# Latent attention scores as three float32r products with operands split one head ahead, and the first norm's steps moved behind the last scale and shift piece

## The chip, the cores and the metric

The kernel runs on one core of one Trainium2 chip. The metric is device microseconds of one execution, as a median over runs. In the rows PE is the matrix engine (TensorE), DVE is VectorE, ACT is ScalarE, POOL is GpSimd, and SP issues most transfers. Matrix products accumulate in eight PSUM banks of 512 float32 columns.

## What is computed

One inference step of a two-layer backbone. 128 context tokens and 256 latent tokens go through the same layers, together 384 columns. A modulation (shift, scale and gate per layer, three times each) is computed from a conditioning vector. Cut to what matters:

```
x += 0.5 * gate1 * SwiGLU1(mod(RMSNorm(x)))
h  = mod(RMSNorm(x));  u = h @ W_in
z  = sig(g_conv)*P_conv(conv) + sig(g_na)*P_na(NA) + sig(g_mla)*P_mla(MLA)
x += gate2 * (z @ W_o)
x += 0.5 * gate3 * SwiGLU2(mod(RMSNorm(x)))
...
prob = softmax(scale * q k^T (+ bias)); o = prob v
```

MLA is attention with 8 heads whose keys are 64 expanded plus 32 rotated dimensions; NA is neighbourhood attention with 8 heads of 64 dimensions and a bias table. Latent queries see 256 latent and 128 cached keys; context queries see the 128 context keys. Everything is float32 in and out.

## The kernel before

The tokens lie in the free dimension (384 columns), features in the partitions. A **dense product** is made of float32r matmuls: the weight is split into a high part (cast on ACT, L320) and a low part (subtraction on DVE, L321), the activation likewise (`split`: cast on ACT L367, subtraction on DVE L368), and three products are added, high·high (L362), low·high activation (L363), high·low weight (L364). Weights come in chunks of 512 KB with 8 blocks of 128x128; `Weights.split` splits a chunk `ahead` chunks (3 as a rule) before PE uses it, and it is called where PE begins a new chunk. `pair` holds the same three products for the FFN's gate and up tiles (L661).

The program is scheduled by hand: on each engine the instructions stand in the order in which the code issues them, and an engine waits at the first whose operands are missing. So the place of a step in the code is its place in each engine's queue.

`first_group` (from L535) computes the first six output tiles of a sublayer with k, the block of 128 features, as the outer loop. It works on features that are not normalised yet, and meanwhile the eight `norm_tile`s of the normalised activation are made in steps: multiply by the inverse RMS (DVE L524), scale and shift (ACT L527, two instructions), then `split` into `hh` and `hl` (ACT L367, DVE L368). `STEPS` says behind which k which tile's next step is issued. In the first sublayer of all, `START_STEPS` says it, and there `start(c)` (c = 0 to 3) also finishes a quarter of the scale and shift vectors: DVE copies it out of PSUM (L402), PE transposes it (L407), DVE reduces it (L408), and ACT and DVE scale two tiles of x by it (L516, L518). `start(3)` stands inside k = 5.

In `attention`, `mla_query(h)` makes a head's query (DVE L957 multiplies it by the rotation) and, for even heads, two heads' keys (ACT copies L962, L963). `scores(heads)` multiplies queries and keys (PE L874 for 2x128 latent queries by 384 keys, L876 for the context), takes the maxima (DVE L889, for NA L885 with the bias), their negative (L890), the exponentials (ACT L895), the reciprocals of the sums (DVE L897) and the probabilities (DVE L902). `transposed` turns them (PE L911, ACT L912), `values` multiplies by v (PE L927, L930; DVE L931). The loop issues, for head i of MLA: scores(i), the query of head i+2, a piece of the convolution (dense tiles on PE, DVE L834 to L850), values of an earlier pair, and transposed(i-1). The NA heads follow in pairs, a pair's two heads side by side in 64-row tiles of PE; `na_values` (L818 to L820) stands behind the first pair. In this kernel the scores are float32 matmuls of q and k as they are; one such matmul leaves two records in the trace.

Of the kernel before, what the change touches and what calls it, by code (L numbers as in the profile page):

```python
# [18 lines left out]
P = 128  # L19
# [27 lines left out]


STEPS = {2: (0, 1, 0, 2, 1, 0), 3: (3, 2, 1, 4, 3, 2), 4: (5, 4, 3, 6, 5, 4), 5: (7, 6, 5, 7), 6: (6,), 7: (7,)}
START_STEPS = {4: (0, 1, 0, 2, 1, 0), 5: (3, 2, 1, 4, 3, 2), 6: (5, 4, 3, 6, 5, 4), 7: (7, 6, 5, 7, 6, 7)}  # L50


START = {0: 0, 1: 1, 3: 2, 5: 3}
# [222 lines left out]
class Weights:  # L276
# [53 lines left out]
    def next(self, n=1):  # L330
        u, b = divmod(self.n, BPC)
        if b == 0:
            self.split(u + self.ahead)
            self.parts.pop(u - 1, None)
        assert b + n <= BPC
        self.n += n
        return tuple(x[:, b * P:(b + n) * P] for x in self.parts[u])
# [7 lines left out]
def step_kernel(ctx, tc, xT, cc, wst, cst_d, vec_d, rpb, ck_na, cv_na, ck_kv, ck_r, yd, o_k, o_v, o_ckv, o_kr):  # L345
# [8 lines left out]
    def wt(n=TOK):  # L354
        return base.tile([P, TOK], F32, tag="w", bufs=8, name="w")[:, :n]

    def small(n, dtype=F32):
        return base.tile([P, 16], dtype, tag="small", bufs=16, name="small")[:, :n]
# [122 lines left out]
    nc.scalar.copy(ones_r, ones)  # L481

    def split_squares():
        sums[:] = [base.tile([P, TOK], F32R, tag=x, name=x) for x in ("sqh", "sql")]
        split(sums[0], sums[1], sumsq[0])

    def add_square(t, last=False):
# [45 lines left out]
    def first_group(l, idx, pool=None):  # L533

        steps = START_STEPS if pool else STEPS
        at_rms = 3 if pool else 1
        if pool:  # L540
            cz = pool.tile([P, KD, 32], F32, name="cz")
            nc.vector.memset(cz, 0.0)
            nc.scalar.activation(cz[:, :, 0:2], vec[:, V_C:V_BADA].rearrange("p (k v) -> p k v", v=2), AF.Silu)
        rest = {}

        def start(c):
            for finish in rest.pop(c):
                finish()
            scales(0, 0, slice(2 * c, 2 * c + 2))
            if c == 0:  # L550
                W.split(0)
            for t in (2 * c, 2 * c + 1):
                scaled(t)
            if c < 2:
                add_square(2 * c)
                add_square(2 * c + 1)

        out = [ps() for _ in range(GROUP)]
        for k in range(KD):
            if pool and k in START:  # L560
                rest[START[k]] = [start_quarter(m, START[k], cz) for m in (1, 0)]
                if k == 0:
                    start(0)
            for j, o in enumerate(out):
                if pool and k % 2 and k < KD - 1 and j == 2:
                    W.prepare()
                    start(k // 2 + 1)
                mm3(o[:, :TOK + 2], W.next(), (hh[:, k, :], hl[:, k, :]), k == 0, k == KD - 1)
            if pool and k == 2:
                for t in range(4, KD):  # L570
                    add_square(t)
                split_squares()
            if k == at_rms:
                rb = inverse_rms()
                tiles = [norm_tile(l, idx, t, rb) for t in range(KD)]
            for t in steps.get(k, ()):
                next(tiles[t])
        b = small(2 * GROUP)
        for j, o in enumerate(out):
            nc.vector.tensor_copy(b[:, 2 * j:2 * j + 2], o[:, TOK:TOK + 2])  # L580
        return out, rb, b
# [145 lines left out]
    def attention(l, h, pool, o_conv, o_na, o_mla):  # L727
# [126 lines left out]

        probs, probsT, queries, mla, na = {}, {}, {}, {}, {}

        def scores(heads):


            near = heads[0] >= 8  # L860
            scale = 1.0 if near else MLA_SCALE
            operands, tiles = [], []
            for i in heads:
                if near:
                    r, j = slice(64 * (i % 2), 64 * (i % 2) + 64), i % 8 // 2
                    operands.append((qna[r, j, :], kna[r, j, :]))
                else:
                    operands.append((queries.pop(i), mla["k"][:, i % 4, :]))
                s = ps(), ps()
                tiles.append((s[0][:, :TOK], s[1][:, :TOK], s[0][:, TOK:]))  # L870
            for j in range(3):
                for (q, k), s in zip(operands, tiles):
                    if j < 2:
                        nc.tensor.matmul(s[j], q[:, NCTX + j * P:NCTX + (j + 1) * P], k[:, NCTX:], start=True, stop=True)  # L874
                    else:
                        nc.tensor.matmul(s[2], q[:, :NCTX], k[:, :NCTX], start=True, stop=True)  # L876
            cols = [slice(0, TOK), slice(TOK, 2 * TOK), slice(2 * TOK, 2 * TOK + NCTX)]
            n = 3 * len(heads)
            mx, nm, sm, rs = small(n), small(n), small(n), small(n)
            for a, (i, s) in enumerate(zip(heads, tiles)):  # L880
                probs[i] = pool.tile([P, 2 * TOK + NCTX], F32, tag="prob", bufs=2, name="prob")
                for j in range(3):
                    m = mx[:, 3 * a + j:3 * a + j + 1]
                    if near and j < 2:
                        nc.vector.tensor_tensor_reduce(  # L885
                            out=probs[i][:, cols[j]], in0=s[j], in1=biases[i % 8][:, j, :], scale=1.0, scalar=-3.0e38,
                            op0=ALU.add, op1=ALU.max, accum_out=m)
                    else:
                        nc.vector.tensor_reduce(m, s[j], axis=AX.X, op=ALU.max)  # L889
            nc.vector.tensor_scalar(nm, mx, -scale, None, op0=ALU.mult)  # L890
            for a, (i, s) in enumerate(zip(heads, tiles)):
                for j in range(3):
                    c = 3 * a + j
                    src = probs[i][:, cols[j]] if near and j < 2 else s[j]
                    nc.scalar.activation(probs[i][:, cols[j]], src, AF.Exp, bias=nm[:, c:c + 1], scale=scale,  # L895
                                         accum_out=sm[:, c:c + 1])
            nc.vector.reciprocal(rs, sm)  # L897
            for a, i in enumerate(heads):
                for j in range(3):
                    c = 3 * a + j  # L900
                    p = probs[i][:, cols[j]]
                    nc.vector.tensor_scalar(p, p, rs[:, c:c + 1], None, op0=ALU.mult)  # L902
                biases.pop(i - 8, None)
# [40 lines left out]
        def mla_query(hd):  # L944


            if hd == 0:
                k = mla["k"] = pool.tile([P, 4, ALLK], F32, tag="A8", bufs=3, name="kmla")

                kr = ps()  # L950
                nc.tensor.matmul(kr, cst[0:64, C_PM:C_MASK], R, start=True, stop=True)
                nc.scalar.copy(k[0:64, 0::2, :], kr[0:64, :].unsqueeze(1).to_broadcast([64, 2, ALLK]))
                nc.scalar.copy(k[64:128, 1::2, :], kr[64:128, :].unsqueeze(1).to_broadcast([64, 2, ALLK]))
            o = dense_tile((cqh, cql), 2)
            q = pool.tile([P, TOK], F32, tag="qmla", bufs=3, name="qmla")
            cs = cst[:, C_CSO:C_CSK] if hd % 2 else cst[:, C_CSE:C_CSO]
            nc.vector.tensor_tensor(q, o[:, :TOK], cs, op=ALU.mult)  # L957
            queries[hd] = q
            if hd % 2 == 0:
                o = ps()  # L960
                mm3(o, W.next(), (ckh, ckl), True, True)
                nc.scalar.copy(mla["k"][64:128, hd % 4, :], o[64:128, :])  # L962
                nc.scalar.copy(mla["k"][0:64, hd % 4 + 1, :], o[0:64, :])  # L963

        mla_values()
        mla_query(0)
        mla_query(1)
        for i in range(8):
            scores([i])
            if i + 2 < 8:  # L970
                mla_query(i + 2)
            if i == 6:
                bias([0, 1])
            for _ in range(FILL[i]):
                next(conv)
            if i >= 3 and i % 2:
                values(i - 3)
            if i >= 1:
                transposed(i - 1)
        for i in range(8, 18, 2):  # L980
            if i > 8:
                transposed(i - 2)
                transposed(i - 1)
            if i < 16:
                scores([i, i + 1])
                if i < 14:
                    bias([i - 6, i - 5])
            if i == 8:
                transposed(7)
                na_values()  # L990
            for _ in range(FILL[i]):
                next(conv)
            values(i - 2)
# [64 lines left out]
```

## Time and profile before

| | us |
|---|---|
| median of 3 runs | 1905.04 (1904.65 to 1905.15) |
| the profiled execution | 1904.49 |
| its span | 1902.7 |
| PE busy | 1875.3 (99%) |
| DVE busy | 1312.3 (69%) |
| ACT busy | 813.2 (43%) |

The mean granted clock of PE was 0.996. A timeline row gives start, duration (of the group, if it counts several), engine, line, operation, output and inputs, count, and in brackets the idle time before it with what ended that. A group of instructions that run one behind the other is one row. Rows overlap: the next PE row begins before the last has drained, so the price of a matmul is the distance between starts, not its duration.

### The profile page before, as it was taken

What the parts mean: (1) busy time and instruction counts of PE and PEld (TensorE: products, weight loads), DVE (VectorE), ACT (ScalarE), POOL (GpSimd) and SP (SyncE); (2) the same over time, 40 slices, a digit from 0 to 9 for tenths busy, and PEclk for the clock granted to TensorE, in tenths of its full rate; (3) what the DMA queues carried; (4) which work ended last, traced back from release to release, by engine and by line L of the source; (5) the groups of instructions that cost most, each with busy time, mean ns of one, the idle gap of its engine ahead of it and who ended that gap; (6) DMA issues with size and microseconds to landing.
All of it is one profiled execution on the core that took longest, in us unless ns stands there. A gap on an engine that the chain in (4) does not pass through costs nothing.

```text
span 1902.7 us, 27717 instructions
## 1 busy us (share of the span) xinstructions
PE 1875.3 (99%) x10804; PEld 1824.2 (96%) x10804; DVE 1312.3 (69%) x2235; ACT 813.2 (43%) x1358; POOL 45.1 (2%) x79
## 2 busy tenths in 40 slices
PE   6999999999999999999999999999999999999998
PEld 5999999988999999999999999998789999999997
DVE  6788767665877778776778776666578766744433
ACT  4633334655533354333354333356554334633332
POOL 0000000013000000000000000000220000000000
PEclk9999999999999999999999999999999999999999
DMA  7567554423455535655535664533335643343331
GB/s 304 190 230 227 198 178 151 130 79 111 144 191 174 196 106 181 219 198 188 178 122 195 206 207 169 186 108 118 101 100 175 205 163 122 112 140 122 127 125 63
DMA packets 85523, 306.12 MB, mean 161 GB/s; under 512 B 9616, under 2 KB 11248, under 8 KB 85264
## 3 DMA queue, kind: packets, MB, share of 16 engines
q1 hardware_dynamic: 83376, 297.21, 46.8%
q0 software_dynamic: 1728, 5.41, 1.0%
q8 instruction: 84, 1.38, 0.3%
q10 hardware_dynamic: 288, 1.74, 0.3%
q14 instruction: 47, 0.39, 0.1%
HBM read 301.53 MB, written 2.79 MB: 160 GB/s over the span
## 4 chain that ended last, share of the span: by engine, by line
PE 93%; DVE 3%; ACT 2%; issue 1%; DMA 0%; SPq 0%; DVEq 0%; ACTq 0%
PE ps L661 34%; PE ps L363 18%; PE ps L362 18%; PE ps L364 18%; PE ps L874 1%; PE ps L911 1%; PE ps L927 1%; PE ps L820 1%; PE ps L818 1%; PE ps L819 1%; ACT w L527 1%; ACT prob L895 0%; DVE lo L321 0%; DVE small L889 0%; ACT hi L320 0%
## 5 line engine op out<-in xcount | busy, mean ns | idle before, releaser
L321 DVE TENSOR_TENSOR lo<-raw,hi 128x1024 fp32r<-128x1024 f32 x414 | 504.8, 1223 | 245.6 <-ACT hi L320 243.9
L320 ACT CAST hi<-raw 128x1024 fp32r<-128x1024 f32 x414 | 429.7, 1046 | 361.6 <-PE ps L363 230.8
L362 PE MATMUL ps<-hh,hi 128*128 128x384 f32 (+1 forms) x960 | 327.4, 341 | 1.9 <-ACT hh L516 1.4
L363 PE MATMUL ps<-hl,hi 128*128 128x384 f32 (+1 forms) x960 | 326.5, 340 | 2.4 <-DVE hl L368 1.8
L364 PE MATMUL ps<-hh,lo 128*128 128x384 f32 (+1 forms) x960 | 325.9, 339 | 0.0
L424 DVE SCALAR_TENSOR_TENSOR junk<-rawa,cb 128x1024 bf16<-128x1024 f32 x256 | 312.9, 1222 | 4.4
L661 PE MATMUL ps<-hl,hi 128*128 128x384 f32 x1216 | 312.6, 338 | 0.0
L661 PE MATMUL ps<-hh,lo 128*128 128x384 f32 x1216 | 312.1, 338 | 0.0
L661 PE MATMUL ps<-hh,hi 128*128 128x384 f32 x1216 | 310.3, 336 | 0.0
L364 PE MATMUL ps<-ah,lo 128*128 128x384 f32 x704 | 237.8, 338 | 0.0
L362 PE MATMUL ps<-ah,hi 128*128 128x384 f32 x704 | 237.8, 338 | 0.0
L363 PE MATMUL ps<-al,hi 128*128 128x384 f32 x704 | 237.8, 338 | 0.0
L661 PEld LDWEIGHTS ps<-hh,lo 128*128 128x128 f32 x1216 | 221.7, 188 | 0.0
L661 PEld LDWEIGHTS ps<-hh,hi 128*128 128x128 f32 x1216 | 221.3, 188 | 0.0
L661 PEld LDWEIGHTS ps<-hl,hi 128*128 128x128 f32 x1216 | 220.1, 188 | 0.0
L362 PEld LDWEIGHTS ps<-hh,hi 128*128 128x128 f32 x960 | 182.2, 190 | 5.5 <-ACT hh L516 1.8
L363 PEld LDWEIGHTS ps<-hl,hi 128*128 128x128 f32 x960 | 181.7, 189 | 3.6 <-DVE hl L368 2.3
L364 PEld LDWEIGHTS ps<-hh,lo 128*128 128x128 f32 x960 | 182.1, 190 | 0.0
L362 PEld LDWEIGHTS ps<-ah,hi 128*128 128x128 f32 x704 | 132.2, 188 | 0.0
L364 PEld LDWEIGHTS ps<-ah,lo 128*128 128x128 f32 x704 | 132.2, 188 | 0.0
L363 PEld LDWEIGHTS ps<-al,hi 128*128 128x128 f32 x704 | 132.2, 188 | 0.0
L638 ACT ACTIVATE w<-ps 128x384 f32<-128x384 f32 x76 | 37.2, 490 | 165.4 <-PE ps L661 165.4
(193 smaller groups left out, 1909.1 us busy)
## 6 DMA issues: line engine op xcount, KB each, us to landing
raw<-wst SPq DMA_DIRECT2D x414, 512.0 KB, 3.4
rawa<-wst SPq DMA_DIRECT2D x128, 512.0 KB, 3.4
s<-wst SPq DMA_DIRECT2D x16, 512.0 KB, 10.0
bias<-rpb POOLq DMA_DIRECT2D x16, 256.0 KB, 3.3
X<-xT SPq DMA_DIRECT2D x4, 384.0 KB, 9.5
y<-X SPq DMA_DIRECT2D x3, 512.0 KB, 3.9
cb<-cc ACTq DMA_DIRECT2D x1, 1024.0 KB, 6.8
cst<-cst ACTq DMA_DIRECT2D x1, 672.0 KB, 4.8
```

Source lines behind the costliest of these rows:

```text
L320: nc.scalar.copy(hi, raw)
L321: nc.vector.tensor_tensor(lo, raw, hi.bitcast(F32), op=ALU.subtract)
L362: nc.tensor.matmul(out, w[0], x[0], start=start, stop=False)
L363: nc.tensor.matmul(out, w[0], x[1], start=False, stop=False)
L364: nc.tensor.matmul(out, w[1], x[0], start=False, stop=stop)
L424: nc.vector.scalar_tensor_tensor(junk, w, 1.0, cb[:, v], op0=ALU.mult, op1=ALU.mult, accum_out=mods[l][:, m, t, v:v + 1])
L527: nc.scalar.activation(h[:, sl], h[:, sl], AF.Identity, bias=mods[l][:, 3 * idx, t, s:s + 1], scale=A[0][:, t, s:s + 1])
L638: nc.scalar.activation(s, g[:, :TOK], AF.Silu)
L661: nc.tensor.matmul(o[:, :TOK], w[part], y, start=k == 0 and i == 0, stop=k == KD - 1 and i == 2)
L818: nc.tensor.matmul(o, xh, wh, start=k == 0, stop=False)
L819: nc.tensor.matmul(o, xl, wh, start=False, stop=False)
L820: nc.tensor.matmul(o, xh, wl, start=False, stop=k == KD - 1)
```

## The change

Four edits. The norm steps of the very first group (`START_STEPS`) begin after k = 5 instead of after k = 4. In the other first groups the chunk split that stood between the last norm steps is put behind the loop (`W.ahead`). The sums of squares use the ring of work tiles (`wt`). The latent scores are made of three float32r products each; a new `prepare(heads)` casts and subtracts query (256 columns) and key (384 columns) one head, or one pair, ahead of its scores. The context scores stay as they are.

```diff
-START_STEPS = {4: (0, 1, 0, 2, 1, 0), 5: (3, 2, 1, 4, 3, 2), 6: (5, 4, 3, 6, 5, 4), 7: (7, 6, 5, 7, 6, 7)}
+START_STEPS = {5: (0, 1, 0, 2, 1, 0, 3), 6: (2, 1, 4, 3, 2, 5, 4, 3, 6), 7: (5, 4, 7, 6, 5, 7, 6, 7)}
...
-        sums[:] = [base.tile([P, TOK], F32R, tag=x, name=x) for x in ("sqh", "sql")]
+        sums[:] = [wt().bitcast(F32R) for _ in range(2)]
...
+            if not pool and k == KD - 2:
+                W.ahead = AHEAD - 1
...
+        if not pool:
+            W.ahead = AHEAD
...
+        def prepare(heads):
+            i = heads[0]
+            if i >= 8:
+                q, k = qna[:, i % 8 // 2, :], kna[:, i % 8 // 2, :]
+                rows = [slice(64 * e, 64 * e + 64) for e in range(2)]
+            else:
+                q, k = queries.pop(i), mla["k"][:, i % 4, :]
+                rows = [slice(0, P)]
+            qs = [pool.tile([P, NLAT], F32R, tag="sq", bufs=4, name="sq") for _ in range(2)]
+            ks = [wt().bitcast(F32R) for _ in range(2)]
+            split(*qs, q[:, NCTX:])
+            split(*ks, k[:, NCTX:])
+            ready[i] = [(q[r], k[r], [x[r] for x in qs], [x[r] for x in ks]) for r in rows]
...
-            for j in range(3):
-                for (q, k), s in zip(operands, tiles):
-                    if j < 2:
-                        nc.tensor.matmul(s[j], q[:, NCTX + j * P:NCTX + (j + 1) * P], k[:, NCTX:], start=True, stop=True)
-                    else:
-                        nc.tensor.matmul(s[2], q[:, :NCTX], k[:, :NCTX], start=True, stop=True)
+            for j in range(2):
+                for n, (a, b) in enumerate(((0, 0), (1, 0), (0, 1))):
+                    for (_, _, q, k), s in zip(operands, tiles):
+                        nc.tensor.matmul(s[j], q[a][:, j * P:(j + 1) * P], k[b], start=n == 0, stop=n == 2)
+            for (q, k, _, _), s in zip(operands, tiles):
+                nc.tensor.matmul(s[2], q[:, :NCTX], k[:, :NCTX], start=True, stop=True)
...
         mla_query(0)
+        prepare([0])
         mla_query(1)
         for i in range(8):
+            prepare([i + 1] if i < 7 else [8, 9])
             scores([i])
...
+            if i < 14:
+                prepare([i + 2, i + 3])
             if i < 16:
                 scores([i, i + 1])
```

How this moves instructions, at three places. On DVE in the very first group, around k = 5 (L524 is a norm step, the two L402 the copies out of PSUM that `start(3)` begins with); before:

```order
L321 TENSOR_TENSOR lo_403<-raw_186,hi_402 128x1024
L524 TENSOR_TENSOR w_426<-X_64,rb_389 128x384
L524 TENSOR_TENSOR w_428<-X_64,rb_389 128x384
L524 TENSOR_TENSOR w_432<-X_64,rb_389 128x384
L368 TENSOR_TENSOR hl_74<-w_426,hh_73 128x384
L402 COPY w_447<-ps_438 128x256
L402 COPY w_458<-ps_449 128x256
L321 TENSOR_TENSOR lo_467<-raw_242,hi_466 128x1024
```

and of the change:

```order
L321 TENSOR_TENSOR lo_403<-raw_186,hi_402 128x1024
L402 COPY w_435<-ps_426 128x256
L402 COPY w_446<-ps_437 128x256
L321 TENSOR_TENSOR lo_455<-raw_242,hi_454 128x1024
L408 TENSOR_REDUCE mod0_71<-ps_460 128x4
L389 TENSOR_TENSOR mod0_71<-mod0_71,vec_65 128x4
```

Three multiplications and one subtraction that stood ahead of the copies now stand behind the whole of `start(3)`.

On ACT at the end of the mixers' first group (L527 and L367 belong to the last two norm tiles, L320 is a chunk's cast); before:

```order
L527 ACTIVATE w_3104<-w_3104,mod0_71,A_2086 128x128
L527 ACTIVATE w_3104<-w_3104,mod0_71,A_2086 128x256
L320 CAST hi_3124<-raw_2994 128x1024
L367 CAST hh_73<-w_3074 128x384
L367 CAST hh_73<-w_3104 128x384
L320 CAST hi_3173<-raw_3048 128x1024
```

and of the change:

```order
L527 ACTIVATE w_3104<-w_3104,mod0_71,A_2086 128x128
L527 ACTIVATE w_3104<-w_3104,mod0_71,A_2086 128x256
L367 CAST hh_73<-w_3074 128x384
L367 CAST hh_73<-w_3104 128x384
L320 CAST hi_3167<-raw_2994 128x1024
L320 CAST hi_3173<-raw_3048 128x1024
```

The chunk's cast changed places with the last two casts of the norm; the subtractions on DVE follow the same order.

On DVE in attention, from the first query to the first probabilities' sum (`sq` and `w` are the low parts of query and key; lines of the change are 17 higher from `scores` on); before:

```order
L957 TENSOR_TENSOR qmla_3477<-ps_3470,cst_66 128x384
L321 TENSOR_TENSOR lo_3490<-raw_3353,hi_3489 128x1024
L957 TENSOR_TENSOR qmla_3498<-ps_3485,cst_66 128x384
L889 TENSOR_REDUCE small_3505<-ps_3500 128x1
L889 TENSOR_REDUCE small_3505<-ps_3501 128x1
L889 TENSOR_REDUCE small_3505<-ps_3500 128x1
L890 TENSOR_SCALAR small_3506<-small_3505 128x3
```

and of the change:

```order
L974 TENSOR_TENSOR qmla_3477<-ps_3470,cst_66 128x384
L368 TENSOR_TENSOR sq_3486<-qmla_3477,sq_3485 128x256
L368 TENSOR_TENSOR w_3488<-kmla_3465,w_3487 128x384
L321 TENSOR_TENSOR lo_3498<-raw_3353,hi_3497 128x1024
L974 TENSOR_TENSOR qmla_3506<-ps_3493,cst_66 128x384
L368 TENSOR_TENSOR sq_3509<-qmla_3506,sq_3508 128x256
L368 TENSOR_TENSOR w_3511<-kmla_3465,w_3510 128x384
L906 TENSOR_REDUCE small_3525<-ps_3516 128x1
L906 TENSOR_REDUCE small_3525<-ps_3517 128x1
L906 TENSOR_REDUCE small_3525<-ps_3516 128x1
L907 TENSOR_SCALAR small_3526<-small_3525 128x3
```

Two subtractions per head stand ahead of the maxima of the head before; on ACT two casts stand likewise ahead of its exponentials.

## Rows read from the trace of the kernel before

**Rows 1.** The page: busy time of each engine.
```profile
PE 1875.3 (99%) x10804; PEld 1824.2 (96%) x10804; DVE 1312.3 (69%) x2235; ACT 813.2 (43%) x1358; POOL 45.1 (2%) x79
```

**Rows 2.** Timeline of PE in the first group.
```profile
47.29 1.12 PE L407 MATMUL ps<-cst,w 128*128 128x128 f32 x4 [5.36 <-DVE w L402]
```

**Rows 3.** Timeline of DVE in the same stretch.
```profile
43.40 1.49 DVE L524 TENSOR_TENSOR w<-X,rb 128x384 f32<-128x384 f32 x3
...
46.82 0.75 DVE L402 COPY w<-ps 128x256 f32<-128x256 f32 x2
...
61.52 1.23 DVE L321 TENSOR_TENSOR lo<-raw,hi 128x1024 fp32r<-128x1024 f32 x1
```

**Rows 4.** Timeline of ACT in the same stretch.
```profile
44.05 1.86 ACT L527 ACTIVATE w<-w,mod,A 128x128 f32<-128x128 f32 x4 [7.94 <-DVE w L524]
...
60.44 2.94 ACT L320 CAST hi<-raw 128x1024 fp32r<-128x1024 f32 x3
```

**Rows 5.** Windows: length, busy and count of PE, PEld, DVE, ACT, POOL; PEclk, DMA.
```profile
46.00:52.00 6.00, 4.71 (x16) 4.68 (x17) 5.22 (x16) 3.88 (x9) 0.00 (x0) 0.50 0.28 96
...
373.00:430.00 57.00, 56.30 (x332) 47.60 (x332) 38.57 (x98) 32.13 (x80) 4.83 (x8) 1.00 0.23 76
430.00:500.00 70.00, 70.00 (x431) 60.12 (x430) 45.18 (x113) 38.58 (x93) 15.25 (x25) 1.00 0.35 113
```

**Rows 6.** The chain of waits: its longest piece (start, us).
```profile
58.81 159.85 PE ps L661 x912
```

**Rows 7.** Timeline of all engines at the end of the mixers' first group.
```profile
339.16 1.03 ACT L320 CAST hi<-raw 128x1024 fp32r<-128x1024 f32 x1
...
340.08 0.33 PE L364 MATMUL ps<-hh,lo 128*128 128x384 f32 x1
340.10 0.92 ACT L367 CAST hh<-w 128x384 fp32r<-128x384 f32 x2
...
340.66 0.44 PE L362 MATMUL ps<-hh,hi 128*128 128x384 f32 x1 [0.24 <-ACT hh L367]
...
341.37 1.02 DVE L368 TENSOR_TENSOR hl<-w,hh 128x384 fp32r<-128x384 f32 x2
...
341.97 0.44 PE L363 MATMUL ps<-hl,hi 128*128 128x384 f32 x1 [0.87 <-DVE hl L368]
```

**Rows 8.** Timeline of PE: scores of an MLA head, then of an NA pair.
```profile
410.19 1.46 PE L874 MATMUL ps<-kmla,qmla 128*128 128x384 f32 x4
411.48 0.38 PE L876 MATMUL ps<-kmla,qmla 128*128 128x128 f32 x2
...
450.29 1.56 PE L874 MATMUL ps<-kna,qna 64*128 64x384 f32 x8
```

**Rows 9.** Waits of DVE from 373 to 430 us: in total, times, longest.
```profile
DVE small L897 <- ACT prob L895: 13.2, 8, 1.7
DVE lo L321 <- ACT hi L320: 3.7, 4, 2.3
DVE small L889 <- PE ps L876: 1.2, 1, 1.2
```

**Rows 10.** Timeline of DVE: subtractions of 128 and of 384 columns.
```profile
363.04 0.28 DVE L368 TENSOR_TENSOR ckl<-ckc,ckh 128x128 fp32r<-128x128 f32 x1
...
365.29 1.02 DVE L368 TENSOR_TENSOR cql<-w,cqh 128x384 fp32r<-128x384 f32 x2
```

**Rows 11.** Timeline of ACT: the second key copy of the first two heads.
```profile
373.26 0.58 ACT L963 COPY kmla<-ps 64x512 f32<-64x512 f32 x1
```

**Rows 12.** Timeline of DVE: maxima of the first and of the last MLA head.
```profile
376.43 1.21 DVE L889 TENSOR_REDUCE small<-ps 128x1 f32<-128x384 f32 x3
...
425.52 1.21 DVE L889 TENSOR_REDUCE small<-ps 128x1 f32<-128x384 f32 x3
```

**Rows 13.** Timeline of PE: the first NA pair's scores, and the last MLA head's transposes.
```profile
428.26 0.59 PE L874 MATMUL ps<-kna,qna 64*128 64x384 f32 x1 [0.69 <-ACT prob L895]
...
429.37 0.96 PE L911 MATMUL ps<-cst,prob 128*128 128x128 f32 x7
```

More of the change, by code (lines that the diff above doesn't have):

```diff
@@ L855, in attention @@
         probs, probsT, queries, mla, na = {}, {}, {}, {}, {}
+        ready = {}
+        def prepare(heads):
[11 more added lines that the diff above has]
+            ready[i] = [(q[r], k[r], [x[r] for x in qs], [x[r] for x in ks]) for r in rows]
         def scores(heads):
@@ L861, in scores @@
             scale = 1.0 if near else MLA_SCALE
-            operands, tiles = [], []
+            operands, tiles = ready.pop(heads[0]), []
             for i in heads:
-                if near:
-                    r, j = slice(64 * (i % 2), 64 * (i % 2) + 64), i % 8 // 2
-                    operands.append((qna[r, j, :], kna[r, j, :]))
-                else:
-                    operands.append((queries.pop(i), mla["k"][:, i % 4, :]))
                 s = ps(), ps()
                 tiles.append((s[0][:, :TOK], s[1][:, :TOK], s[0][:, TOK:]))
-            for j in range(3):
-                for (q, k), s in zip(operands, tiles):
-                    if j < 2:
-                        nc.tensor.matmul(s[j], q[:, NCTX + j * P:NCTX + (j + 1) * P], k[:, NCTX:], start=True, stop=True)
-                    else:
-                        nc.tensor.matmul(s[2], q[:, :NCTX], k[:, :NCTX], start=True, stop=True)
+            for j in range(2):
[4 more added lines that the diff above has]
+                nc.tensor.matmul(s[2], q[:, :NCTX], k[:, :NCTX], start=True, stop=True)
             cols = [slice(0, TOK), slice(TOK, 2 * TOK), slice(2 * TOK, 2 * TOK + NCTX)]
```

## Prediction

> **What bounds the kernel now.** I read the page first: PE is busy for 1875.3 us, 99% of the span [rows 1]. So there is little idle time to win, and a change gains only where it closes one of PE's gaps or takes time out of PE's own work. I then looked along PE's timeline for gaps, and at what ended each. The longest of the first group is at 47.29 us: PE stands 5.36 us until DVE has copied a quarter of the modulation out of PSUM [rows 2]. Two short ones stand at the end of the mixers' first group, at 340.66 and 341.97, and both recur in the second layer [rows 7]. The third place is attention, 373 to 430 us. There PE is busy 56.30 of 57 us and DVE only 38.57 [rows 5], which looks as if PE alone counted. The waits of DVE say otherwise: of its 18 us idle, 13.2 are eight waits for the exponentials, and only one wait of 1.2 us is for scores from PE [rows 9]. So seven of the eight heads' maxima begin when DVE's own queue lets them, with the scores already there. DVE with ACT's exponentials is a second loop as long as PE's, in the order of a hand schedule; PE runs ahead of it by small margins. What is put into that loop moves every later head.
>
> **The very first group.** Before, the copies L402 begin at 46.82, behind three L524 that begin at 43.40 and a subtraction that waits for ACT [rows 3]. Now they take the place of the first L524: 46.82 - 43.40 = 3.42 us earlier, and with them L407, so PE's idle time falls from 5.36 to 1.94. Before, the granted clock was 0.50, the lower level, from 46 to 52 us, behind the idle stretch [rows 5]; I take it that after 1.94 us it does not fall. The gain does not last to the end of the norm, however. While PE stood, ACT did scale and shift of two tiles, 1.86 us [rows 4], and a cast, .41 (what the second of two adds [rows 7]), together some 2.2; this work now comes behind `start(3)`, on an engine with the other norm tiles queued, and the chunk cast that PE needs next stands behind all of them (the x3 group at 60.44 [rows 4]). Of the 3.4 - 2.2 = 1.2 the new pipe's first multiplication takes .65 before ACT can begin (43.40 to 44.05 [rows 3, 4]). That cast and the subtraction at 61.52 [rows 3] so come about .6 earlier. PE needs them for the fifth k of its next pair of tiles. Before, the group ended at 58.81 [rows 6] and four k took 4 x 6 x .175 = 4.2 us (.175 = 159.85/912 [rows 6]): 63.0, later than the subtraction's end, 61.52 + 1.23 = 62.75, so there was no wait, and the fifth k ended at 63.0 + 1.05 = 64.05. Now PE would be at the fifth k some 5 us earlier and waits about 3.3 for the cast and again for the low part, at 62.75 - .6 = 62.15; two more passes, .35, and the fifth k ends at 62.5. Net: **-1.5 us**. Bounds: -5 (the chunk is no obstacle) and +1.5 (the clock falls in the new idle time: six us at half speed lose 3.0 [rows 5]).
>
> **The other first groups.** In the mixers a chunk's cast begins at 339.16 and the last two norm casts only at 340.10; behind them DVE does the chunk's low part first, and the last L368 only from 341.37 [rows 7]. Start to start PE loses (340.66 - 340.08 - .17) + (341.97 - 340.66 - .17) = .41 + 1.14 = 1.55, and .1 in the slower first passes behind each gap. With the casts at 339.16, both high parts are there by 340.1 and the low ones by 340.8, when PE wants them at 340.2 and 340.4 for one k after the other; I count the gaps as gone. The split that is put behind has three chunks of lead. In the FFN's first groups PE has no such gap, so nothing is won there. **-1.65 per layer, -3.3.** Bounds -3.5 and -1.5.
>
> **PE's saving in the scores.** Four records of an MLA head take 411.48 - 410.19 = 1.29 us start to start, .3225 each [rows 8]; six float32r passes of 384 columns take 6 x .175 = 1.05. So a head saves .24. An NA pair's eight records last 1.56 where an MLA head's four last 1.46 [rows 8]: the two 64-row tiles run side by side. If the float32r ones do too, a pair saves .24. Over 16 heads and 8 pairs that is 5.8 us at most. A float32 matmul is two records, .645, which is 3.7 float32r passes. The Trainium skill, "FP8 and Floating Point Precision", section TensorE Precision Notes, says that float32 takes four passes (high and low parts, all four products); by it the saving would be .70 - .525 = .175 instead of .12 a matmul, 48 x .055 = 2.7 us more, and the sum 1910.7; the row decides, and it says .645.
>
> **The price of the preparation.** Two subtractions of 384 take 1.02, the second adding .47 to the first's .55; one of 128 takes .28, .20 without its drain [rows 10]. So 256 columns cost .34 and a head's two subtractions **.81 us** on DVE. On ACT two casts of 384 take .92 [rows 7], so a head's two about .8, in the time in which it waits for the maxima anyway; that I cost at nothing, except at head 0. There query and keys exist only from 373.26 + .58 on [rows 11], so the first casts end about 374.6 and the key's low part about 375.2, where PE began the scores about 373.6: +1.1 for PE with its saving counted. On DVE two preparations, 1.62, and this delay stand ahead of head 0's maxima: about +2.1 on 376.43 [rows 12]. Each of the next seven heads finds one more preparation ahead of it: 7 x .81 = 5.7. The only idle time in front of maxima, 1.2 us [rows 9], takes up about .9. So head 7's maxima move from 425.52 [rows 12] by 2.1 + 5.7 - .9 = 6.9 us, and its exponentials and probabilities with them. PE already waited .69 for those exponentials at 428.26 (a PSUM bank), and its transposes of head 7 come right behind at 429.37 [rows 13]: they have no margin and move by 6.9. One output tile of `na_values` takes a bank that the first pair's maxima free, .45 more. PE: **+7.35 per layer, +14.7**; its own saving in the eight heads disappears in these waits. The bounds: nothing but the saving less head 0's wait, 8 x .24 - 1.1 = -.8 per layer, and 8 x .81 + 2.1 = +8.6. I take the upper part because DVE shows no other idle time that a preparation could fall into: those 13.2 us stand inside each head's softmax, behind the place of the preparation. Where it goes ahead of the maxima, it cannot use them. Among the NA pairs DVE and ACT are less loaded against PE's dense work (45.18 and 38.58 of 70 us, PE 70.00 [rows 5]), so there only PE's saving shows: three pairs, -.7 per layer, **-1.5**.
>
> **The sum.** 1904.49 - 1.5 - 3.3 + 14.7 - 1.5 = 1912.9 for the profiled execution; the median of the runs stands .55 above it, so **1913.4**.
>
> **The rivals.** *PE alone counts* (faster, .15): the subtractions fall into DVE's 18 idle us and delay nobody. For it: PE is busy 98.8% of that stretch [rows 5]. Against it: the waits [rows 9]. It decides at the point where DVE idles ahead of the maxima, waiting for PE: if the scores come last there, a preparation is free. Then -1.5 - 3.3 - 5.8 + 2 x 1.1 = -8.4: 1896.6. *The 64-row float32r tiles don't run side by side* (.10): a pair then needs 12 x .175 = 2.10 against 1.05, +1.05 for six pairs beyond the waits, +6.3: 1919.7. No row shows such a pair; the float32 ones speak against it [rows 8]. *The clock falls again* in the first group or in an attention wait of 2 us or more (.08): +3.0, 1916.4. *Half the delay* is taken up by L321's waits for ACT, 3.7 us in that stretch [rows 9] (.07): 1913.4 - 7.35 = 1906.
>
> **How the numbers follow.** The forecast has .60, with 1909 to 1917 as its own range (the bounds of the first two edits, and one us per layer in the loop). The range 1904 to 1921 takes in all but the rival in which PE alone counts. A measurement of this kernel can tell .2%, 3.8 us, from no change: faster is below 1901.2, slower above 1908.8. Faster has .15; the half delay and the forecast's low end make .10 for the same; slower has .75.
>
> **What would show it.** In the profile of the changed kernel L407 should begin near 43.9 with about 1.9 us idle, and PE should wait some 3 us for `lo` of L321 in the first pair behind the group; the two gaps of the mixers' group should be gone. In attention, DVE should wait for PE's scores in none or one head, PE should wait several times for ACT's exponentials or copies and for DVE's probabilities, together about 8 us per layer, and a head's maxima should begin behind its successor's subtractions. If DVE waits for PE in most heads, the loop theory is wrong. If NA scores of a pair take 2.1 us, the second rival is right.

## The result, and the profile after

The changed kernel takes **1919.38 us** (median, 1918.76 to 1920.08) against 1904.85 us of the kernel before beside it: a ratio of 1.0077, with an interval of 1.006 to 1.0095. It is slower, by 14.5 us where the forecast was 8.5; the time lies within the range of 1904 to 1921, near its upper end, and above the forecast's own 1909 to 1917. (Of the kernel with float32 scores below one execution is left out: it took 2293 us at a granted clock of .75 from end to end.)

The page of the changed kernel: PE's work hardly grew, its share of the span fell. The last line is the chain of work that ended last; below it stands that of the kernel before, in which DVE and ACT had less.

```profile
span 1918.0 us, 27947 instructions
...
PE 1879.9 (98%) x10868; PEld 1836.0 (96%) x10868; DVE 1334.7 (70%) x2283; ACT 830.5 (43%) x1406; POOL 45.4 (2%) x79
...
PE 89%; DVE 5%; ACT 3%; DMA 1%; issue 1%; SPq 0%; DVEq 0%; ACTq 0%
```
```profile
PE 93%; DVE 3%; ACT 2%; issue 1%; DMA 0%; SPq 0%; DVEq 0%; ACTq 0%
```

To see where the 15.3 us of span went, I took five stretches between the same instructions of PE in each trace. The marks are the first product with the sums of squares (L448), the FFN's first down product, the two small products at the head of attention (`R`, L951, now L968), the start of the last `values` of layer 0, and the same two places of layer 1.

| stretch, us | before | changed | difference | forecast |
|---|---|---|---|---|
| first group and FFN | 183.37 | 183.45 | +.1 | -1.5 |
| down products and mixers' first group | 151.07 | 149.40 | -1.67 | -1.65 |
| attention, layer 0 | 125.94 | 135.99 | +10.05 | +6.6 |
| between the two layers' attention | 802.29 | 800.65 | -1.64 | -1.65 |
| attention, layer 1 | 125.83 | 134.91 | +9.08 | +6.6 |

(The forecast's 6.6 is 7.35 for the loop less .72 for three pairs.) The five differences add up to 15.9; the other -.6 lies ahead of the first mark (-.4) and behind the last (-.2). So the split's edit gave what it was to give, the start gave nothing, and attention cost half as much again as forecast.

**The very first group.** PE's and ACT's timelines of the changed kernel:

```profile
43.45 0.77 PE L407 MATMUL ps<-cst,w 128*128 128x128 f32 x4 [1.94 <-DVE w L402]
...
60.52 0.62 PE L665 MATMUL ps<-hh,hi 128*128 128x384 f32 x2 [2.05 <-ACT hi L320]
...
61.78 0.69 PE L665 MATMUL ps<-hh,lo 128*128 128x384 f32 x1 [0.26 <-DVE lo L321]
```
```profile
59.43 2.93 ACT L320 CAST hi<-raw 128x1024 fp32r<-128x1024 f32 x3
```

The idle time in front of L407 is 1.94 us, as worked out, where it was 5.36 [rows 2]; the wait for the chunk has come in its place, as the prediction had it (2.05 and .26 us, where it said 3.3), and the chunk's cast begins 1.0 us earlier than before [rows 4]: the .6 of the forecast, and .4 by which this execution was ahead already at the products with the sums of squares (34.71 against 35.12 us). What the sum had put at nothing is the clock. The windows over the two waits:

```profile
43.50:48.00 4.50, 4.50 (x18) 4.38 (x19) 4.21 (x15) 1.49 (x4) 0.00 (x0) 0.62 0.73 228
60.00:66.00 6.00, 5.23 (x20) 4.88 (x21) 5.71 (x14) 3.31 (x6) 0.00 (x0) 0.72 0.84 304
```

Mean granted clocks of .62 and .72 mean that a part of each window, behind its wait of 2 us, ran at the lower of the two levels.

**The mixers' first group.** ACT's timeline: the last two norm casts now stand ahead of the chunks', and PE waits for nothing from 330 to 366 us.

```profile
338.85 0.91 ACT L367 CAST hh<-w 128x384 fp32r<-128x384 f32 x2
339.66 2.00 ACT L320 CAST hi<-raw 128x1024 fp32r<-128x1024 f32 x2
```

**Attention.** DVE's waits from 371 to 439 us, then PE's:

```profile
DVE small L914 <- ACT prob L912: 13.2, 8, 1.7
DVE sq L368 <- ACT sq L367: 2.4, 3, 1.7
DVE lo L321 <- ACT hi L320: 1.8, 4, 0.5
```
```profile
PE ps L944 <- ACT probT L929: 4.1, 2, 2.5
PE ps L891 <- ACT prob L912: 2.0, 1, 2.0
PE ps L891 <- ACT w L367: 0.9, 1, 0.9
PE ps L891 <- DVE sq L368: 0.8, 1, 0.8
PE ps L362 <- ACT prob L912: 0.3, 1, 0.3
```

DVE still waits eight times for the exponentials, 13.2 us, to the tenth what it was [rows 9]: the preparation used none of that time. The one wait for PE's scores is gone. PE in turn waits 8.1 us, where it waited .7. The maxima of the first and the last head on DVE's timeline, with the last head's preparation:

```profile
376.60 1.21 DVE L906 TENSOR_REDUCE small<-ps 128x1 f32<-128x384 f32 x3
...
431.14 0.42 DVE L368 TENSOR_TENSOR sq<-qna,sq 128x256 fp32r<-128x256 f32 x1
431.47 0.55 DVE L368 TENSOR_TENSOR w<-kna,w 128x384 fp32r<-128x384 f32 x1
431.94 1.21 DVE L906 TENSOR_REDUCE small<-ps 128x1 f32<-128x384 f32 x3
```

Attention begins 2.0 us earlier (367.56 against 369.56), so head 0 is late by 376.60 - 376.43 + 2.0 = 2.2 us and head 7 by 431.94 - 425.52 + 2.0 = 8.4 [rows 12]. Forecast were 2.1 and 6.9.

### The profile page after: what moved, and what is told of

Read it like the earlier page. It is cut to its first block, busy times and chain, and to the rows that moved or that the text cites. A ratio compares the mean times of both kernels' runs of the same rounds, so it can differ in the third digit from the quotient of the medians.

```text
span 1918.0 us, 27947 instructions
## 1 busy us (share of the span) xinstructions
PE 1879.9 (98%) x10868; PEld 1836.0 (96%) x10868; DVE 1334.7 (70%) x2283; ACT 830.5 (43%) x1406; POOL 45.4 (2%) x79
## 3 DMA queue, kind: packets, MB, share of 16 engines
q8 instruction: 85, 1.39, 0.3%
## 4 chain that ended last, share of the span: by engine, by line
PE 89%; DVE 5%; ACT 3%; DMA 1%; issue 1%; SPq 0%; DVEq 0%; ACTq 0%
PE ps L665 33%; PE ps L362 17%; PE ps L363 17%; PE ps L364 17%; ACT prob L912 1%; DVE small L906 1%; DMA s<-wst 1%; PE ps L928 1%; DVE lo L321 1%; PE ps L944 1%; PE ps L822 1%; PE ps L823 1%; PE ps L824 1%; ACT hi L320 1%; DMA X<-xT 1%
## 5 line engine op out<-in xcount | busy, mean ns | idle before, releaser
L320 ACT CAST hi<-raw 128x1024 fp32r<-128x1024 f32 x414 | 429.9, 1046 | 368.5 <-PE ps L363 229.6
## 6 DMA issues: line engine op xcount, KB each, us to landing
s<-wst SPq DMA_DIRECT2D x16, 512.0 KB, 10.1
```

The source lines that it names most:

```text
L320: nc.scalar.copy(hi, raw)
```

## The experiments

Two theories. **The loop:** what costs the time is the place of the subtractions on DVE, ahead of the maxima, in a loop that is as long as PE's. **The rival:** the new products, ACT's casts or the clock cost it, wherever the subtractions stand. Eight kernels tell them and the parts apart; three more try what follows. "Attention" below is the stretch of the table, layer 0 and layer 1.

**The start's order alone** (on the kernel before):

```diff
-START_STEPS = {4: (0, 1, 0, 2, 1, 0), 5: (3, 2, 1, 4, 3, 2), 6: (5, 4, 3, 6, 5, 4), 7: (7, 6, 5, 7, 6, 7)}
+START_STEPS = {5: (0, 1, 0, 2, 1, 0, 3), 6: (2, 1, 4, 3, 2, 5, 4, 3, 6), 7: (5, 4, 7, 6, 5, 7, 6, 7)}
```

> Kernel before (1904.85 us) with the new order of the first norm's steps alone. As the traces of before and after read: the wait in front of the transposes falls from 5.4 to about 1.9 us, but the clock falls behind it all the same, and PE then waits some 2 us for the chunk that ACT casts behind the eight norm tiles: 1904.0 to 1905.5, no gain. By my prediction's own step: 1903.4. If the wait were simply gone: 1901 or less.

Measured: 1904.46 against 1904.29 us, ratio 1.0001 (.9991 to 1.0011): nothing. Its trace is the more telling, since here the clock kept the higher level behind the first wait:

```profile
43.00:48.00 5.00, 4.11 (x21) 3.41 (x22) 4.71 (x16) 1.50 (x4) 0.00 (x0) 1.00 0.56 193
58.00:66.00 8.00, 4.93 (x18) 4.62 (x19) 7.06 (x16) 5.42 (x10) 0.00 (x0) 0.79 0.76 243
```
```profile
60.77 0.62 PE L661 MATMUL ps<-hh,hi 128*128 128x384 f32 x2 [2.90 <-ACT hi L320]
```

PE was at the chunk sooner and waited for it .85 us longer than in the changed kernel; the clock fell behind that wait. Counted from the first mark, PE goes on at 25.8 us in both traces, so the chunk sets that moment, however fast the group runs. In the kernel before, PE began the same products at 27.7 us without a wait (62.84 - 35.12); the 1.9 us are gone again by the end of the stretch (183.64 against 183.37), behind the lower clock (.79 over 8 us).

**The split alone** (on the kernel before):

```diff
+            if not pool and k == KD - 2:
+                W.ahead = AHEAD - 1
...
+        if not pool:
+            W.ahead = AHEAD
```

> Kernel before with the chunk split of the later first groups put behind the loop, and nothing else. If the two gaps in the mixers' group are only this split's place in the queue, both go in both layers: 4 x .4 to 1.2, -3.3, 1901.5. Rival: the split that is now late is waited for behind the loop, in the next tiles, and the time stays at 1904.8.

Measured: 1901.09 us, ratio .9983 (.9974 to .9993), 3.2 us less. The split that comes late is not waited for: PE has no wait from 330 to 366 us, nor at the same place of layer 1.

**The scores and their preparation alone** (the changed kernel with the first two edits undone):

```diff
-START_STEPS = {5: (0, 1, 0, 2, 1, 0, 3), 6: (2, 1, 4, 3, 2, 5, 4, 3, 6), 7: (5, 4, 7, 6, 5, 7, 6, 7)}
+START_STEPS = {4: (0, 1, 0, 2, 1, 0), 5: (3, 2, 1, 4, 3, 2), 6: (5, 4, 3, 6, 5, 4), 7: (7, 6, 5, 7, 6, 7)}
...
-            if not pool and k == KD - 2:
-                W.ahead = AHEAD - 1
```

> The changed kernel with the first two edits undone: float32r scores and their preparation alone. If the parts add up and attention alone loses: 1919.4 + 3.3 = 1922.7, within 1 us. If part of the loss comes from the start or the split of the first groups: nearer to 1915.

Measured: 1924.89 us, ratio 1.0108 (1.0093 to 1.0123), 20.6 us more than before. By the marks above attention takes 136.02 and 135.97 us, +10.1 in each layer; in the stretches from the FFN's down products to attention and between the layers nothing changed (151.05 and 802.29). The third edit, the work tiles for the sums of squares, is in this kernel too and shows no price there. The time is 2.2 us above the expected 1922.7, out of its 1 us. In the profiled executions 1.2 us of the difference from the changed kernel lie ahead of the first mark, where both do the same work, and 1.1 in attention of layer 1, whose loss so varies between executions.

**The same work in another place** (on the changed kernel): the casts stay ahead of the exponentials, the subtractions go behind them on DVE.

```diff
-            split(*qs, q[:, NCTX:])
-            split(*ks, k[:, NCTX:])
+            pairs = ((qs, q[:, NCTX:]), (ks, k[:, NCTX:]))
+            for x, full in pairs:
+                nc.scalar.copy(x[0], full)
+
+            def low():
+                for x, full in pairs:
+                    nc.vector.tensor_tensor(x[1], full, x[0].bitcast(F32), op=ALU.subtract)
+
+            lows.append(low)
...
+            while lows:
+                lows.pop()()
             nc.vector.reciprocal(rs, sm)
...
         prepare([0])
+        lows.pop()()
```

> The changed kernel with the same casts, subtractions and products, but the two subtractions of the next head stand behind the exponentials, where DVE waits 1.65 us per head for ACT (head 0's stay where they are). If DVE's order is the cause: .8 of the 1.65 us is filled, the heads follow each other as in the kernel before, and 1901 to 1903 is left (the split's -3.3, the NA pairs' -1.5, some +1 per layer from head 0). If the float32r products, ACT's casts or the clock are the cause: 1915 or more.

Measured: 1901.53 us, ratio .9985 (.9976 to .9995): 17.9 us less than the changed kernel, with the same instructions. DVE's timeline of a head, and its waits from 371 to 430 us:

```profile
384.30 0.17 DVE L914 TENSOR_SCALAR small<-small 128x3 f32<-128x3 f32 x1
384.37 0.42 DVE L881 TENSOR_TENSOR sq<-qmla,sq 128x256 fp32r<-128x256 f32 x1
384.71 0.55 DVE L881 TENSOR_TENSOR w<-kmla,w 128x384 fp32r<-128x384 f32 x1
386.12 0.18 DVE L923 RECIPROCAL small<-small 128x3 f32<-128x3 f32 x1 [0.86 <-ACT prob L919]
```
```profile
DVE small L923 <- ACT prob L919: 7.1, 8, 1.7
```

The wait for the exponentials shrank from 1.65 to .86 us at this head, by the subtractions' .81, and over the eight heads from 13.2 to 7.1. Attention takes 126.78 and 125.67 us. That settles the loop against the rival: products, casts and subtractions are all there, and the loss is gone. (The two kernels ran in different sittings; the kernel before took 1904.29 us beside this one and 1904.85 beside the changed one, so .6 of the 17.9 may be the sitting's.)

**The preparation without the products** (on the changed kernel):

```diff
-                for n, (a, b) in enumerate(((0, 0), (1, 0), (0, 1))):
-                    for (_, _, q, k), s in zip(operands, tiles):
-                        nc.tensor.matmul(s[j], q[a][:, j * P:(j + 1) * P], k[b], start=n == 0, stop=n == 2)
+                for (q, k, _, _), s in zip(operands, tiles):
+                    nc.tensor.matmul(s[j], q[:, NCTX + j * P:NCTX + (j + 1) * P], k[:, NCTX:], start=True, stop=True)
```

> The changed kernel with its preparation (both casts and both subtractions per head, in the same places), but the scores are the float32 matmuls of before and don't read what was prepared. If the preparation's place on DVE is the cause, nearly all of the loss stays: 1917 to 1921 (the NA pairs' saving of 1.5 lost, the waits of head 0 and of the first pair for their operands gone). If the float32r products cost the time: 1904 or less.

Measured: 1921.57 us, ratio 1.0088 (1.0071 to 1.0105). The loss stays without any float32r score, .6 above what was expected.

**The products without the subtractions** (on the changed kernel). The high parts stand in for the low ones, so this kernel computes other scores, with the same casts and products:

```diff
-            qs = [pool.tile([P, NLAT], F32R, tag="sq", bufs=4, name="sq") for _ in range(2)]
-            ks = [wt().bitcast(F32R) for _ in range(2)]
-            split(*qs, q[:, NCTX:])
-            split(*ks, k[:, NCTX:])
-            ready[i] = [(q[r], k[r], [x[r] for x in qs], [x[r] for x in ks]) for r in rows]
+            qs = [pool.tile([P, NLAT], F32R, tag="sq", bufs=4, name="sq")]
+            ks = [wt().bitcast(F32R)]
+            nc.scalar.copy(qs[0], q[:, NCTX:])
+            nc.scalar.copy(ks[0], k[:, NCTX:])
+            ready[i] = [(q[r], k[r], [qs[0][r]] * 2, [ks[0][r]] * 2) for r in rows]
```

> The changed kernel without the subtractions on DVE: the high parts stand in for the low parts of query and key, ACT's casts and PE's six products a head stay. If DVE's two subtractions a head are the cause: 1899 to 1902, as with the hidden ones or a little less. If ACT's casts ahead of the exponentials do it: 1915 or more.

Measured: 1903.35 us, ratio .9994 (.9985 to 1.0004): 16.0 us less than the changed kernel, though 1.4 above what was expected. ACT's casts are all still there, so the subtractions are nearly the whole price. What the 1.4 us above the expectation are is open; in the trace attention takes 125.31 us in layer 0 and 127.36 in layer 1, and the granted clock fell to the lower level in that of layer 1 alone.

**Without POOL's mask additions** (on the changed kernel; the mask is left out of the bias tables):

```diff
-            for hd in heads:
-                for qt in range(2):
-                    d = biases[hd][:, qt, 0:NLAT].rearrange("p (r c) -> p r c", r=4)
-                    nc.gpsimd.tensor_tensor(d, d, cst[:, C_MASK:C_END].unsqueeze(1).to_broadcast([P, 4, 64]),
-                                            op=ALU.add)
```

> The changed kernel without POOL's additions of the mask to the bias tables. In its trace the three L919 of head 5 take 2.29 us instead of .95 while POOL adds masks. If POOL's additions hold DVE there: 1.3 per layer less, 1916.7. If it was chance or lies off the path: 1919.4.

Measured: 1916.63 us, ratio 1.0067 (1.0052 to 1.0082): 2.75 us less by the medians, with intervals that overlap. Its execution at a mean granted clock of .995 took 1916.56 us, the changed kernel's at the same clock 1918.96, and attention takes 133.68 and 133.85 us, 2.3 and 1.1 less, of which the clock may have a part. The rows speak more clearly. DVE and POOL of the changed kernel, and DVE of this one (where L914 is the line that is L919 there):

```profile
418.81 2.29 DVE L919 TENSOR_SCALAR prob<-prob,small 128x384 f32<-128x384 f32 x3
421.03 0.54 DVE L974 TENSOR_TENSOR qmla<-ps,cst 128x384 f32<-128x384 f32 x1
```
```profile
418.65 3.06 POOL L753 TENSOR_TENSOR bias<-bias,cst 128x256 f32<-128x256 f32 x4 [2.64 <-DMA bias<-rpb]
```
```profile
418.98 0.94 DVE L914 TENSOR_SCALAR prob<-prob,small 128x384 f32<-128x384 f32 x3
```

Beside POOL's four additions DVE's three probabilities take 2.29 us, without them .94. The next DVE instruction, which reads PSUM and one SBUF tile, keeps its .54 while the last addition still runs. In the kernel before, the additions ran from 416.6 to 419.4 us, beside maxima, which read PSUM and kept their 1.22 us, and in DVE's wait for the exponentials.

**One chunk more split ahead in the start** (on the changed kernel):

```diff
+            if pool and k == KD - 2:
+                W.ahead = 2
```

> The changed kernel with one chunk more split ahead in the last two k of the very first group, so that the cast that PE waited for at 60.5 us stands ahead of the last norm tiles. If that place in ACT's queue gives back the start's gain: the wait of 2.4 + .6 us and the lower clock behind it go, 1919.4 - 3 to 4 = 1915.9. If the norm tiles then come late instead: 1918 to 1919.4.

Measured: 1917.98 us, ratio 1.0069 (1.0054 to 1.0084): 1.4 less than the changed kernel by the medians, not to be told from it by the intervals. The first stretch takes 183.10 us against 183.45, which tells nothing: among kernels with one and the same start it differs by 1 us. The wait for the chunk is gone, and another has taken its place, on the next pair's PSUM tiles, which DVE frees (L650):

```profile
65.06 0.88 PE L667 MATMUL ps<-hh,hi 128*128 128x384 f32 x2 [1.69 <-DVE w L650]
```

The clock kept its higher level from 44 to 66 us and fell behind this wait (.62 from 66 to 70.5 us).

**What follows for a better kernel.** The split's edit and the start's order of before, with float32r scores for the NA pairs alone (MLA heads float32) and their subtractions behind the exponentials; the diff is against the kernel with the subtractions there, and heads that nothing was prepared for take the float32 matmuls:

```diff
-        prepare([0])
...
-            prepare([i + 1] if i < 7 else [8, 9])
+            if i == 7:
+                prepare([8, 9])
             scores([i])
```

> The split edit, float32 scores for the MLA heads as before, float32r scores for the NA pairs alone, with their subtractions behind the exponentials; the start's order as before. The parts add up: 1904.5 - 3.3 (split) - 1.5 (six pairs beyond the waits) = 1899.7. If the pairs' preparation delays something among the NA pairs: 1901 or more.

Measured: **1899.82 us**, ratio .9975 (.9966 to .9984), 4.7 us less than the kernel before, as expected, and the fastest here. Attention takes 125.08 and 125.01 us. Then head 0's scores ahead of the second query:

```diff
         mla_query(0)
+        scores([0])
         mla_query(1)
```

> As b1_near, and head 0's scores and softmax are issued ahead of the second query, so that its maxima no longer stand behind a chunk's subtraction (DVE waited 2.3 us there) and DVE's loop begins some 2 us earlier. If DVE's loop sets the wait of 1.0 us for the first NA pair's bank in each layer, that goes: 1897.7. If PE's own work is all that is left: 1899.7.

Measured: 1901.61 us, ratio .9985 (.9976 to .9994): a miss. PE's waits from 366 to 440 us name two, and DVE's from 371 to 430 show its loop ahead of PE now:

```profile
PE ps L905 <- DVE sq L881: 0.7, 1, 0.7
PE ps L901 <- ACT kmla L995: 0.7, 1, 0.7
```
```profile
DVE small L920 <- PE ps L907: 4.9, 3, 2.6
```

Head 0's scores wait for ACT's key copies; the first pair's wait for operands, whose subtractions stand in head 7's softmax, is in the kernel without this edit too (.8 us). So the edit bought a wait of .7 us a layer, and attention takes 125.95 and 126.15 us, .9 and 1.1 more. DVE waits for PE three times, 4.9 us, where it waited once, 1.2 [rows 9]: an earlier start of its loop is of no use there. With MLA heads 1 to 7 in float32r too:

```diff
         mla_query(1)
+        prepare([1])
+        lows.pop()()
         for i in range(8):
-            if i == 7:
-                prepare([8, 9])
             if i:
+                prepare([i + 1] if i < 7 else [8, 9])
                 scores([i])
```

> As b3_early, and the MLA heads 1 to 7 have float32r scores too, with their subtractions behind the exponentials of the head before. If the loop has the slack that b3_early gives it, PE's saving shows: 14 heads x .24 = 3.4 us less than b3_early, 1894.3. If the loop still sets the pace: the time of b3_early, 1897.7, or more.

Measured: 1904.51 us, ratio .9999 (.999 to 1.0008): a miss again. One preparation, head 1's, is not hidden in it, and PE waits 1.1 us for the first pair's operands. Why it is 2.9 us above the kernel without float32r in the MLA heads is not settled. The granted clock goes with it: attention takes 126.15 us in layer 0, .2 more, but 127.62 in layer 1, 1.5 more, and there alone the granted clock fell; its six executions at a mean clock of .995 took 1904.5 to 1905.3 us, its five at .996 to .998 1901.8 to 1903.5.

## Why the prediction was right, and where its sum was off

**The bound.** That DVE's loop paces the MLA heads and PE follows was right: the same instructions behind the exponentials give back 17.9 us, and taking the subtractions away gives back 16.0. (In both figures is also what the later loop brought with it, POOL's additions and the clock, below.) The rival "PE alone counts" decided at the point where DVE waits for scores, and after the change it waits for none.

**The loop's price** was the mis-sized term: +7.35 per layer forecast, +10.8 and +9.8 measured (10.05 and 9.08, with three pairs' .72 added back). Head 0's late scores and two preparations were right (2.2 against 2.1), as was .8 for each of the next heads (1 to 3 are late by 3.0, 3.8 and 4.6), and the 1.2 us for which head 5's maxima had waited for scores took up nearly all of one preparation (head 4 is late by 5.58, head 5 by 5.63). Two things were left out. *POOL:* the later loop brought DVE's probabilities of head 5 beside POOL's mask additions, 2.29 - .95 = 1.34 us in layer 0 and 1.91 - .95 = .96 in layer 1. With that head 7 is late by 8.4 and 8.25 us, where 6.9 was forecast. That a delayed engine meets something else was to be asked at that place, and was not. *The clock:* between 430.4 and 437.7 PE was busy 4.52 of 7.30 us, and its clock fell. The windows of that stretch and the next, PE's rows in them, and the same products before:

```profile
430.40:437.70 7.30, 4.52 (x24) 3.46 (x24) 5.54 (x16) 3.16 (x10) 0.00 (x0) 0.70 0.08 31
437.70:440.30 2.60, 2.60 (x8) 2.12 (x8) 2.21 (x11) 0.32 (x1) 1.67 (x4) 0.52 0.14 16
```
```profile
436.36 1.76 PE L928 MATMUL ps<-cst,prob 128*128 128x128 f32 x7
437.77 0.78 PE L822 MATMUL ps<-hi,hh 128*128 128x512 f32 x1
...
440.58 0.40 PE L823 MATMUL ps<-hi,hl 128*128 128x512 f32 x1
```
```profile
430.08 0.48 PE L818 MATMUL ps<-hi,hh 128*128 128x512 f32 x1
...
431.81 0.39 PE L819 MATMUL ps<-hi,hl 128*128 128x512 f32 x1
```

Head 7's transposes take 437.77 - 436.36 = 1.41 us start to start, where they took 430.08 - 429.37 = .71 [rows 13], and the first seven products of `na_values` 440.58 - 437.77 = 2.81, where they took 431.81 - 430.08 = 1.73: 1.8 us together, and 1.5 in layer 1. The last .6 of layer 0 lie between head 7's maxima and its transposes (4.42 us against 3.85), while PE does the pair's last scores at the lower clock. So 8.4 + .6 + 1.8 make the 10.8, and 8.25 + 1.5 the 9.8. The forecast's .45 for a bank that `na_values` waits for is not there: it follows the transposes without a wait in both kernels. The prediction had the clock's fall as a rival of .08, for one of two places; it came at both.

**The start:** the step "I take it that after 1.94 us it does not fall" failed, in two ways. Six traces with this order have that wait of 1.9 us; the clock fell behind it in two, the changed kernel's and that without masks, and not in the four others. And it fell behind the wait for the chunk in all five that have one, which the prediction named but did not charge with a lower clock. -1.5 was forecast; the edit alone measured +.2, with an interval of .1% (1.9 us) either way, which by itself would leave room for -1.5. The first stretch does not: in six traces with the old order it takes 182.75 to 183.80 us, in five with the new one 182.90 to 183.68.

**The first groups:** -3.3 forecast, -3.2 measured alone, -1.67 and -1.64 by the marks.

**The NA pairs:** the float32r tiles of 64 rows do run side by side. Twelve products take 460.23 - 459.07 = 1.16 us start to start, where eight records took 1.39:

```profile
459.07 1.32 PE L891 MATMUL ps<-w,sq 64*128 64x384 f32 x12
460.23 0.39 PE L893 MATMUL ps<-kna,qna 64*128 64x128 f32 x4
```

That is .23 a pair against a forecast .24. An MLA head saves less than the .24 worked out: its six products take 1.15 us (from 1353.39 to 1354.54), not 1.05; in those heads the saving goes into the waits either way. The prediction's side sum of 1910.7 takes .055 off at all 48 matmuls, while its main sum counts PE's saving for six pairs alone: 12 x .055 = .7, and 1912.7.

**Where it was luck.** The direction and its cause were right, the size was not: the misses of the loop (5.9 us) and of the start (1.6) have one sign, and only the wide range, not the forecast's own, holds the time. And the measured 1919.38 is all but the 1919.7 of the rival whose 64-row tiles don't run side by side. That mechanism is not there: a pair takes 1.16 us and not 2.1. Who had the time alone could have believed it.

## What to carry to other kernels

An engine that is busy two thirds of the time can still set the pace, if it works in order and its idle time lies inside a chain: look at which wait its idle time is, and put new work behind the instruction that starts that wait, not ahead of the chain. Here the place alone of two subtractions a head was worth some 17 us. Where PE must wait longer, ask also what the delayed engines then meet (another engine's reads and writes) and what the clock does behind the wait.

## What the runs showed that was not expected

DVE's multiplications from SBUF to SBUF (the probabilities) took more than twice their time while POOL added masks, 2.29 us for three against .94; POOL's four additions took 3.06 us against 2.82 in the kernel before. The Trainium skill, "SBUF — State Buffer", section "SBUF: two separate sides", says that a DVE operation in a two-port mode and a GpSimd operation share one pair of ports under a lock, and that whichever starts second is blocked for the other's whole instruction. The trace fits that, without showing the ports: the ends of POOL's additions and of DVE's probabilities alternate from 419.4 to 421.7 us. Further, behind waits of the same 1.94 us in the first group the granted clock fell in one execution (.62 over 4.5 us) and not in another (1.00 over 5 us), so a wait of that length is no sure price either way.
